# Strassen's seven products in the second MLP matrices of a two-layer decoder trunk, with weight sums formed by accumulating DMAs

## The chip, the core and the metric

The kernel runs on one core of one Trainium2 chip. A core has a matrix engine (TensorE, PE in the profile, with its weight loads as PEld), three engines for elementwise work (VectorE as DVE, ScalarE as ACT, GpSimd as POOL), and SyncE (SP), which here only issues DMAs. DMAs can also be issued from the ACT and POOL queues. The metric is the device time of one execution in microseconds (us); less is better.

## The reference

Two layers over a residual stream x of 256 tokens by 2048 columns, in float32. Layer 0 mixes tokens with gated linear attention, layer 1 with sliding-window attention. Behind each mixer stands the same MLP, with matrices of 2048 x 8192 and 8192 x 2048:

```python
def rmsnorm(x, g):
    xf = x.astype(jnp.float32)
    y = xf * lax.rsqrt(jnp.mean(xf * xf, axis=-1, keepdims=True) + EPS)
    return (y * g.astype(jnp.float32)).astype(x.dtype)

def sqrelu_mlp(h, w1, w2):
    u = jax.nn.relu(h @ w1)
    return (u * u) @ w2

    # in every layer
    h = h + mixer(rmsnorm(h, norm_mix[layer]))
    h = h + sqrelu_mlp(rmsnorm(h, norm_mlp[layer]), mlp_w1[layer], mlp_w2[layer])
```

The change concerns the product with w2, and the square of the ReLU ahead of it. All weights come from HBM once per execution; the four MLP matrices are 256 MiB of them.

## The kernel before: how the work is laid out

**Float32 products by halves.** TensorE is fed with the type float32r. Every float32 operand is split into a high part (a cast) and a low part (what the cast left over), and a product is three matmuls: high x high, high x low, low x high. A weight block of 512 x 512 (1 MiB) is loaded by one DMA from the SP queue into a tile `ws` (`split_w`, line 114; three buffers), and then split in two pieces of 128 x 1024 elements: ScalarE casts to `wh` (line 125), VectorE subtracts to `wl` (line 126). The `wh` and `wl` tiles have four buffers each, which is two blocks. These instructions are put 60 places ahead of program order (`high_priority`), so that blocks are split about two ahead of the matmuls that use them.

**The MLP** (`mlp`, line 666) runs four groups g. A group takes 2048 of the 8192 hidden columns, in two stages:

- The w1 stage: four chunks of 512 hidden columns, each a `gemm_wide` over four blocks (128 matmuls with the weights as the stationary operand). Its result lies hidden column by partition. `evac_u` (line 683) takes it from PSUM: ScalarE copies one half sum and VectorE adds the other (688, 689), GpSimd multiplies by the norm scale of the token (694), VectorE computes max(m, 0) * m (695), ScalarE casts the high part (696) and GpSimd subtracts the low part (697).
- The w2 stage: four chunks of 512 model columns, each a `gemm_mov` over four blocks, 96 matmuls with the activations as the stationary operand: 4 blocks x 4 slices of 128 rows x 2 halves of the tokens x 3. VectorE adds each 128 x 512 result to the residual `xs` (`add_to`, line 621).

The last group of layer 1 (g = 3 without `gains`) has another w2 stage, with weights as the stationary operand, that ends in the output.

**What orders the work.** Program order with those priorities; every engine and every DMA queue executes its instructions in order. `tick` and `later` place small work of one stage between the matmuls of the next. At the end of layer 0 the `add_to` of each chunk also sums squares for the next norm and makes the operands of layer 1 from the chunk a few ticks later.

Of the kernel before, what the change touches and what calls it, by code (L numbers as in the profile page):

```python
# [16 lines left out]
P = 128  # L17
# [31 lines left out]
def yoco_kernel(ctx: ExitStack, tc: tile.TileContext, x, norms, mlp_w1, mlp_w2, a_w_in, w_glr, w_gate, a_g_o, a_w_o,  # L49
# [12 lines left out]
    def bank(shape, tag, dtype=F32):  # L62
        return ps[tag].tile(shape, dtype, name=tag, tag=tag)
# [7 lines left out]
    def later(n, fn):  # L71
        due.setdefault(now[0] + n, []).append(fn)

    def tick():
        now[0] += 1
        for fn in due.pop(now[0], ()):
            fn()

    def mm(o, l, r, start=True, stop=True, **kw):
        nc.tensor.matmul(o, lhsT=l, rhs=r, start=start, stop=stop, **kw)  # L80
# [20 lines left out]
    nc.gpsimd.memset(mhalf, -0.5)  # L101


    def split_w(parts, step=4, queue=nc.sync, between=None):
        ws = wp.tile([P, 4, C], F32, name="ws", tag="ws", bufs=WS)
        halves = [(wp.tile([P, 2, C], F32R, name="wh", tag="wh", bufs=WHL),
                   wp.tile([P, 2, C], F32R, name="wl", tag="wl", bufs=WHL)) for _ in range(2)]
        with tc.high_priority(offset=WPRI):
            for k in range(0, 4, step):
                ks = slice(k, k + step)  # L110
                o = 0
                for ap in parts:
                    n = ap.shape[1]
                    queue.dma_start(out=ws[:, ks, o:o + n],
                                    in_=ap[k * P:(k + step) * P].rearrange("(k p) n -> p k n", p=P))
                    o += n
            n = min(step, 2)
            for k in range(0, 4, n):
                wh, wl = halves[k // 2]
                js, ks = slice(k % 2, k % 2 + n), slice(k, k + n)  # L120
                with ExitStack() as order:
                    if between:
                        for ins in between(k):
                            order.enter_context(tc.issue_after(ins.ins))
                    h = nc.scalar.copy(out=wh[:, js, :o], in_=ws[:, ks, :o])  # L125
                    l = nc.vector.tensor_sub(out=wl[:, js, :o], in0=ws[:, ks, :o], in1=wh.bitcast(F32)[:, js, :o])  # L126
                if between:
                    last[:] = h, l
        return halves
# [156 lines left out]

    last = []

    ss = sm.tile([P, 2, T], F32, name="ss", tag="ss", bufs=1)
    rstd = sm.tile([P, NT], F32, name="rstd", tag="rstd")  # L290
    rb = sm.tile([P, T], F32, name="rb", tag="rb")
    rbq = sm.tile([P, T], F32, name="rbq", tag="rbq", bufs=1)
    rb4, rbq4 = (a.rearrange("p (o t n) -> p o t n", o=1, t=NT).broadcast_to([P, 2, NT, P]) for a in (rb, rbq))
    sqx = []

# [28 lines left out]
        later(8, lambda: nc.scalar.mul(out=rbq, in_=rb, mul=DK ** -0.5))  # L324


    ga = ExitStack()
    gp = ga.enter_context(tc.tile_pool(name="gp", bufs=1))
    g2 = ga.enter_context(tc.tile_pool(name="g2", bufs=2))


# [76 lines left out]
    def two(a, b):  # L408
        return a[:, :, 2 * b:2 * b + 2].rearrange("p t c n -> p c t n")
# [208 lines left out]
    def add_to(c, acts, gains, sq, r):  # L618

        def evac(t, acc):  # L620
            nc.vector.tensor_add(out=xs[c][:, t], in0=acc, in1=xs[c][:, t])
# [44 lines left out]
    def mlp(w1, w2, act, r, gains):  # L666
        mx = ExitStack()
        mp = mx.enter_context(tc.tile_pool(name="mp", bufs=2))
        rb = sm.tile([P, T], F32, name="rb", tag="rb")
        later(RS + 2, lambda: along(rb, r))  # L670
        rb2 = twice(rb)
        sq, nr = new_norm() if gains else (None, None)
        acts = [[] for _ in gains]
        wide_tags.sort()
        for g in range(4):
            us = []
            for c in range(NC4):
                u = new_act()
                us.append(u)

                ms = {}

                def evac_u(f, acc, u=u, ms=ms):
                    ah, al, _ = u
                    if f % 2 == 0:
                        ms[0] = mp.tile([P, 2, T], F32, name="m", tag="m")
                    m, j = ms[0], f % 2
                    nc.scalar.copy(out=m[:, j], in_=acc[:, 1])
                    nc.vector.tensor_add(out=m[:, j], in0=acc[:, 0], in1=m[:, j])  # L689
# [4 lines left out]
                    nc.gpsimd.tensor_mul(out=m, in0=m, in1=rb2)  # L694
                    nc.vector.scalar_tensor_tensor(out=m2, in0=m, scalar=0.0, in1=m, op0=ALU.max, op1=ALU.mult)  # L695
                    nc.scalar.copy(out=ah[:, bs], in_=m2)  # L696
                    nc.gpsimd.tensor_sub(out=al[:, bs], in0=m2, in1=ah.bitcast(F32)[:, bs])  # L697

                go_all(gemm_wide(piece(w1, g * D + c * C), act, evac_u))
            w = w2[g * D:(g + 1) * D]  # L700
# [252 lines left out]
```

## Time and profile before

| | |
|---|---|
| time, median of 3 runs | 2097.48 us (2097.38 to 2099.07) |
| profiled execution | 2099.51 us, with a span of 2097.8 us |
| instructions in the span | 27171 |
| moved by DMA | 381.20 MB, a mean of 182 GB/s |

The span runs from the first to the last instruction; the profiled execution's own time is 1.7 us longer. In the views, a row of a group names the line of the kernel, the engine, the operation, and the output and input tiles with their shapes; its busy time is in us, the mean of one instruction in ns. A matrix-engine instruction is shown from its start to its modelled end, and successive ones overlap, so its duration is more than its share of the time: how long a stage takes is read from the chain of work that ended last, where each piece carries its start, its length and its number of instructions. The view by stretches gives each engine's busy time in a stretch with the number of instructions, then the granted TensorE clock (1.00 is full), the mean busy share of the 16 DMA engines, and GB/s.

### The profile page before, as it was taken

How to read it: one execution, taken by the hardware profiler on the slowest of the kernel's cores; microseconds unless marked ns; L12 is line 12 of the kernel's file. 1: busy time of each engine (PE TensorE's matmuls, PEld its weight loads, DVE VectorE, ACT ScalarE, POOL GpSimd, SP SyncE). 2: the span in 40 equal slices, each digit the busy share in tenths (PEclk: the TensorE clock that was granted, in tenths of full speed). 3: DMA queues.
4: the chain of work that ended last, by engine and by line, in shares of the span. 5: the costliest groups of instructions: out<-in, count | busy, mean ns of one | idle time of the engine just before them, and what ended most of it. 6: DMA issues, size and time to landing. Idle time of an engine off the chain costs nothing.

```text
span 2097.8 us, 27171 instructions
## 1 busy us (share of the span) xinstructions
PE 2086.2 (99%) x10902; PEld 1772.0 (84%) x10902; DVE 1256.8 (60%) x1335; ACT 1017.0 (48%) x1387; POOL 354.4 (17%) x279
## 2 busy tenths in 40 slices
PE   9999999999999999999999999999999999999999
PEld 9988888888888888888888877788888888888888
DVE  6695444566556556645666677566556655655654
ACT  6645445554344434434455677544434434434442
POOL 2262111022012102201300233012102201300310
PEclk9999999999999999999999999999999999999999
DMA  7445555555555655565565433555655565566553
GB/s 277 143 140 180 180 180 163 178 181 195 189 184 195 197 188 194 183 199 184 180 196 186 151 131 123 178 173 191 199 188 193 182 200 184 178 201 199 181 192 130
DMA packets 195871, 381.20 MB, mean 182 GB/s; under 512 B 6577, under 2 KB 14785, under 8 KB 195745
## 3 DMA queue, kind: packets, MB, share of 16 engines
q1 hardware_dynamic: 194704, 377.51, 55.2%
q8 instruction: 85, 1.39, 0.3%
q10 hardware_dynamic: 720, 1.09, 0.2%
q0 software_dynamic: 320, 0.87, 0.2%
q14 instruction: 42, 0.34, 0.0%
HBM read 377.35 MB, written 2.10 MB: 181 GB/s over the span
## 4 chain that ended last, share of the span: by engine, by line
PE 93%; DVE 3%; ACT 2%; DMA 1%; issue 1%; POOL 0%; ACTq 0%; POOLq 0%; DVEq 0%
PE acc L80 70%; PE ms L80 12%; PE tp L80 10%; ACT sc L846 1%; PE tp L605 1%; DVE wl L126 1%; DMA ws<-in_a_w_in_dram 1%; ACT wh L125 1%; PE tp L779 0%; DVE st L840 0%; DVE st L842 0%; PE tp L555 0%; DVE po L868 0%; DVE pv L868 0%; DMA gk<-in_b_g_q_dram 0%
## 5 line engine op out<-in xcount | busy, mean ns | idle before, releaser
L126 DVE TENSOR_TENSOR wl<-ws,wh 128x1024 fp32r<-128x1024 f32 (+1 forms) x720 | 927.0, 1294 | 713.6 <-ACT wh L125 712.7
L125 ACT CAST wh<-ws 128x1024 fp32r<-128x1024 f32 (+1 forms) x720 | 748.1, 1042 | 886.4 <-PE acc L80 676.3
L80 PE MATMUL acc<-wh,act 128*128 128x512 f32 x3136 | 988.0, 392 | 0.0
L80 PEld LDWEIGHTS acc<-wh,act 128*128 128x128 f32 x3136 | 588.0, 188 | 123.8 <-issue 2.0
L80 PE MATMUL acc<-wl,act 128*128 128x512 f32 x1568 | 610.8, 390 | 0.5 <-DVE wl L126 0.5
L80 PE MATMUL acc<-act,wh 128*128 128x512 f32 (+1 forms) x1664 | 412.8, 362 | 1.0 <-ACT wh L125 0.7
L80 PEld LDWEIGHTS acc<-wl,act 128*128 128x128 f32 x1568 | 294.5, 188 | 61.7 <-issue 1.7
L80 PEld LDWEIGHTS acc<-act,wh 128*128 128x128 f32 x1664 | 279.5, 190 | 28.6 <-ACT wh L125 1.0
L80 PE MATMUL acc<-act,wl 128*128 128x256 f32 x1408 | 256.6, 282 | 0.0
L694 POOL TENSOR_TENSOR m<-m,rb 128x512 f32<-128x512 f32 x64 | 81.8, 1300 | 994.5 <-DVE m L689 994.5
L80 PEld LDWEIGHTS acc<-act,wl 128*128 128x128 f32 x1408 | 226.3, 190 | 25.1 <-DVE wl L126 0.3
L80 PE MATMUL tp<-act,wh 128*128 128x512 f32 x592 | 230.1, 394 | 0.0
L80 PE MATMUL ms<-act,wh 128*128 128x512 f32 x576 | 225.9, 394 | 0.0
L80 PE MATMUL ms<-act,wl 128*128 128x256 f32 x576 | 148.6, 281 | 0.0
L80 PE MATMUL tp<-act,wl 128*128 128x256 f32 x576 | 148.3, 280 | 0.0
L697 POOL TENSOR_TENSOR act<-m,act 128x512 fp32r<-128x512 f32 x64 | 130.7, 2057 | 50.2 <-ACT act L696 50.2
L80 PEld LDWEIGHTS tp<-act,wh 128*128 128x128 f32 x592 | 111.5, 189 | 13.3
L80 PEld LDWEIGHTS ms<-act,wh 128*128 128x128 f32 x576 | 108.6, 189 | 13.6
L80 PEld LDWEIGHTS tp<-act,wl 128*128 128x128 f32 x576 | 108.3, 189 | 12.7
L80 PEld LDWEIGHTS ms<-act,wl 128*128 128x128 f32 x576 | 108.5, 189 | 11.9
L695 DVE SCALAR_TENSOR_TENSOR m<-m 128x512 f32<-128x512 f32 x64 | 84.1, 1344 | 26.4 <-POOL m L694 26.4
L696 ACT CAST act<-m 128x512 fp32r<-128x512 f32 x64 | 39.3, 622 | 48.8 <-DVE m L695 48.8
(185 smaller groups left out, 947.2 us busy)
## 6 DMA issues: line engine op xcount, KB each, us to landing
ws<-in_mlp_w_dram SPq DMA_DIRECT2D x256, 1024.0 KB, 5.1
ws<-in_a_w_in_dram SPq DMA_DIRECT2D x44, 1024.0 KB, 5.0
ws<-in_a_w_o_dram SPq DMA_DIRECT2D x16, 1024.0 KB, 4.9
ws<-in_b_w_q_dram SPq DMA_DIRECT2D x16, 1024.0 KB, 5.0
ws<-in_b_w_o_dram SPq DMA_DIRECT2D x16, 1024.0 KB, 5.0
ws<-in_a_w_in_dram SPq DMA_DIRECT2D x12, 256.0 KB, 6.4
xt<-in_x_dram SPq DMA_DIRECT2D x8, 256.0 KB, 6.6
ws<-in_kv_w_k_dram SPq DMA_DIRECT2D x4, 512.0 KB, 4.3
```

Source lines behind the costliest of these rows:

```text
L80: nc.tensor.matmul(o, lhsT=l, rhs=r, start=start, stop=stop, **kw)
L125: h = nc.scalar.copy(out=wh[:, js, :o], in_=ws[:, ks, :o])
L126: l = nc.vector.tensor_sub(out=wl[:, js, :o], in0=ws[:, ks, :o], in1=wh.bitcast(F32)[:, js, :o])
L605: nc.tensor.transpose(out=tp[:, j, t], in_=xs[c][:, t, (2 * b + j) * P:(2 * b + j + 1) * P], identity=ident)
L694: nc.gpsimd.tensor_mul(out=m, in0=m, in1=rb2)
L695: nc.vector.scalar_tensor_tensor(out=m2, in0=m, scalar=0.0, in1=m, op0=ALU.max, op1=ALU.mult)
L696: nc.scalar.copy(out=ah[:, bs], in_=m2)
L697: nc.gpsimd.tensor_sub(out=al[:, bs], in0=m2, in1=ah.bitcast(F32)[:, bs])
L846: nc.scalar.activation(out=sc[:, h], in_=sc[:, h], func=AF.Exp, bias=nmx[:, h:h + 1], scale=f[:, h:h + 1], accum_out=su[:, h:h + 1])
```

## The change

In both MLPs, all groups but the last of layer 1 (seven of eight) have a new w2 stage. It handles the model columns in two halves n of 1024. A half is a 2 x 2 x 2 product of blocks: the two halves of the tokens, two blocks of 512 hidden columns, two of 512 model columns, summed over two pairs q of hidden blocks. Eight half products become seven, by the Strassen-Winograd form:

- **Activations.** `combine` forms the seven left factors of each pair of hidden chunks: three subtractions on VectorE (`less`), and for every factor a cast on ScalarE and a subtraction on VectorE (`half`), all 128 x 512.
- **Weights.** The seven right factors of a pair q come as a chain of sums in place: `X` holds block (0,0), then + (0,1), then + (1,1), then + (1,0); `Y` holds block (1,1), then + (0,1); block (1,0) is used alone. A first block is a plain load from the SP queue. A block is added by a DMA from the GpSimd queue with `accum_op=ALU.add`, into the tile whose last value has just been split. Each of the 14 values is split by `halve`, which is the loop of `split_w` made a function. `X` has two buffers of its own, `Y` and the single block share `ws`.
- **Products.** `product` is 24 matmuls (2 pairs x 4 slices x 3) into one PSUM bank. Its sum is added to one or two of the four 128 x 512 residual tiles or to a tile `v` that is kept over the groups.
- **The ReLU.** VectorE now computes max(m, 0) * rb, with the norm scale rb, and ScalarE squares the result into a float32 tile `u`. GpSimd no longer takes part. In the group that keeps the old w2 stage the low part is subtracted on VectorE.

Besides, two tiles of the first layer's mixer move to a pool that is released before the MLP. The core of the diff; `halve` is the old loop with the same instructions:

```diff
-                m2 = mp.tile([P, 2, T], F32, name="m2", tag="m2")
-                nc.gpsimd.tensor_mul(out=m, in0=m, in1=rb2)
-                nc.vector.scalar_tensor_tensor(out=m2, in0=m, scalar=0.0, in1=m, op0=ALU.max, op1=ALU.mult)
-                nc.scalar.copy(out=ah[:, bs], in_=m2)
-                nc.gpsimd.tensor_sub(out=al[:, bs], in0=m2, in1=ah.bitcast(F32)[:, bs])
+                nc.vector.scalar_tensor_tensor(out=m, in0=m, scalar=0.0, in1=rb2, op0=ALU.max, op1=ALU.mult)
+                nc.scalar.activation(out=uf[c][:, bs], in_=m, func=AF.Square)
...
+        def combine(op, odd, uf):
...
+            def half(i, a):
+                nc.scalar.copy(out=op[i][:, 0], in_=a)
+                nc.vector.tensor_sub(out=op[i][:, 1], in0=a, in1=op[i].bitcast(F32)[:, 0])
...
+            if not odd:
+                half(0, ua[:, :, :P])
+                half(6, less(ua[:, :, :P], ua[:, :, P:]))
+                return
+            e = less(ua[:, :, P:], ub[:, :, P:])
+            s = less(ua[:, :, :P], e)
+            half(4, e)
+            half(2, less(ub[:, :, :P], s))
+            half(5, s)
+            half(1, ub[:, :, :P])
+            half(3, ub[:, :, P:])
...
+            def load(ws, q, i, j):
+                with tc.high_priority(offset=WPRI):
+                    nc.sync.dma_start(out=ws, in_=block(q, i, j))
+                return ws
+
+            def more(ws, q, i, j):
+                with tc.high_priority(offset=WPRI):
+                    nc.gpsimd.dma_start(out=ws, in_=block(q, i, j), accum_op=ALU.add)
+                return ws
...
+            weights = [lambda q: load(new(X, q), q, 0, 0), lambda q: load(new(Y, q), q, 1, 1),
+                       lambda q: more(X[q], q, 0, 1), lambda q: more(Y[q], q, 0, 1), lambda q: more(X[q], q, 1, 1),
+                       lambda q: load(new({}, q), q, 1, 0), lambda q: more(X[q], q, 1, 0)]
...
+            def product(i, b, o):
...
+                for q in range(2):
+                    halves = halve(weights[i](q))
+                    op = ops[q][o]
+                    for k in range(4):
+                        wh, wl = (h[:, k % 2] for h in halves[k // 2])
+                        st = fresh and q == 0 and k == 0
+                        mm(banks[b], op[:, 0, k], wh, st, False, skip_group_check=True)
+                        mm(banks[b], op[:, 0, k], wl, False, False, skip_group_check=True)
+                        mm(banks[b], op[:, 1, k], wh, False, q == 1 and k == 3, skip_group_check=True)
+                    tick()
+                return banks[b]
...
+            p = product(0, "A", 0)
+            if g == 0:
+                nc.scalar.mul(out=v, in_=p, mul=-1.0)
+            else:
+                sub(v, p)
+            add(x12, product(1, "E", 2))
+            p = product(2, "B", 4)
+            add(x12, p)
+            add(x22, p)
+            sub(x22, product(3, "C", 6))
+            add(v, product(4, "D", 5))
+            if final:
+                add(x12, v)
+                add(x22, v)
+                done(c1)
+                sub(x21, v)
+            add(x11, product(5, "A", 1))
+            add(x21, product(6, "C", 3))
+            if final:
+                done(c0)
...
-            if g < 3 or gains:
-                for c in range(NC4):
-                    go_all(gemm_mov(piece(w, c * C), us, add_to(c, acts, gains if g == 3 else (), sq, nr)))
+            if not plain:
+                for n in range(2):
+                    seven(w, n, ops, g, g == 3 or (g == 2 and not gains), acts, gains if g == 3 else (), sq, nr)
                 continue
```

More of the change, by code (lines that the diff above doesn't have):

```diff
@@ L101, in yoco_kernel, with halve @@
     nc.gpsimd.memset(mhalf, -0.5)
+    def halve(ws, o=C, n=2, between=None, low=None):
+        halves = [(wp.tile([P, 2, C], F32R, name="wh", tag="wh", bufs=WHL),
+                   wp.tile([P, 2, C], F32R, name="wl", tag="wl", bufs=WHL)) for _ in range(2)]
+        with tc.high_priority(offset=WPRI):
+            for k in range(0, 4, n):
+                wh, wl = halves[k // 2]
+                js, ks = slice(k % 2, k % 2 + n), slice(k, k + n)
+                with ExitStack() as order:
+                    if between:
+                        for ins in between(k):
+                            order.enter_context(tc.issue_after(ins.ins))
+                    h = nc.scalar.copy(out=wh[:, js, :o], in_=ws[:, ks, :o])
+                    l = (low or nc.vector).tensor_sub(out=wl[:, js, :o], in0=ws[:, ks, :o],
+                                                      in1=wh.bitcast(F32)[:, js, :o])
+                if between:
+                    last[:] = h, l
+        return halves
     def split_w(parts, step=4, queue=nc.sync, between=None):
         ws = wp.tile([P, 4, C], F32, name="ws", tag="ws", bufs=WS)
-        halves = [(wp.tile([P, 2, C], F32R, name="wh", tag="wh", bufs=WHL),
-                   wp.tile([P, 2, C], F32R, name="wl", tag="wl", bufs=WHL)) for _ in range(2)]
         with tc.high_priority(offset=WPRI):
@@ L116, in split_w @@
                     o += n
[L117 to L129, printed above, removed]
+        return halve(ws, o, min(step, 2), between)
     def piece(w, col, n=C):
@@ L287, in yoco_kernel @@
     last = []
[L289 removed]
     rstd = sm.tile([P, NT], F32, name="rstd", tag="rstd")
     rb = sm.tile([P, T], F32, name="rb", tag="rb")
[L292 removed]
+    ga = ExitStack()
+    gp = ga.enter_context(tc.tile_pool(name="gp", bufs=1))
+    ss = gp.tile([P, 2, T], F32, name="ss")
+    rbq = gp.tile([P, T], F32, name="rbq")
     rb4, rbq4 = (a.rearrange("p (o t n) -> p o t n", o=1, t=NT).broadcast_to([P, 2, NT, P]) for a in (rb, rbq))
@@ L674, in mlp, with new_ops, less @@
         wide_tags.sort()
+        vs = [mp.tile([P, C], F32, name=f"v{n}", bufs=1) for n in range(2)]
+        def new_ops():
+            two = lambda: actp.tile([P, 2, 2, 4, P], F32R, name="ops", tag="act")
+            pairs = [two() for _ in range(2)]
+            return [t[:, i] for t in pairs for i in range(2)] + \
+                [mp.tile([P, 2, 4, P], F32R, name=f"op{i}", tag=f"op{i}") for i in range(3)]
+        def combine(op, odd, uf):
+            ua, ub = (uf[c] for c in sorted(uf)[-2:]) if odd else (uf[max(uf)], None)
+            def half(i, a):
+                nc.scalar.copy(out=op[i][:, 0], in_=a)
+                nc.vector.tensor_sub(out=op[i][:, 1], in0=a, in1=op[i].bitcast(F32)[:, 0])
+            def less(a, b):
+                e = mp.tile([P, 4, P], F32, name="e", tag="e")
+                nc.vector.tensor_sub(out=e, in0=a, in1=b)
+                return e
+            if not odd:
[9 more added lines that the diff above has]
+            half(3, ub[:, :, P:])
@@ new lines, in seven, with block, new, done @@
+        def seven(w, n, ops, g, final, acts, gains, sq, nr):
+            c0, c1 = 2 * n, 2 * n + 1
+            x11, x21, x12, x22 = (xs[c][:, t] for c in (c0, c1) for t in range(NT))
+            v = vs[n]
+            X, Y = {}, {}
+            def block(q, i, j):
+                r = (2 * q + i) * C
+                return w[r:r + C, (c0 + j) * C:(c0 + j + 1) * C].rearrange("(k p) n -> p k n", p=P)
+            def load(ws, q, i, j):
[3 more added lines that the diff above has]
+            def more(ws, q, i, j):
+                with tc.high_priority(offset=WPRI):
+                    nc.gpsimd.dma_start(out=ws, in_=block(q, i, j), accum_op=ALU.add)
+                return ws
+            def new(d, q):
+                if d is X:
+                    d[q] = mp.tile([P, 4, C], F32, name="wx", tag="wx")
+                else:
+                    d[q] = wp.tile([P, 4, C], F32, name="ws", tag="ws", bufs=WS)
+                return d[q]
+            weights = [lambda q: load(new(X, q), q, 0, 0), lambda q: load(new(Y, q), q, 1, 1),
+                       lambda q: more(X[q], q, 0, 1), lambda q: more(Y[q], q, 0, 1), lambda q: more(X[q], q, 1, 1),
+                       lambda q: load(new({}, q), q, 1, 0), lambda q: more(X[q], q, 1, 0)]
+            banks = {}
+            def product(i, b, o):
+                fresh = b not in banks
+                if fresh:
+                    banks[b] = bank([P, C], "ms" if b in "DE" else "acc")
+                for q in range(2):
[9 more added lines that the diff above has]
+                return banks[b]
+            add = lambda o, p: nc.vector.tensor_add(out=o, in0=p, in1=o)
+            sub = lambda o, p: nc.vector.tensor_sub(out=o, in0=o, in1=p)
+            def done(c):
+                if not gains:
+                    return
+                for t in range(NT):
+                    junk = sm.tile([P, C], F32, name="junk", tag="junk", bufs=1)
+                    nc.scalar.activation(out=junk, in_=xs[c][:, t], func=AF.Square, accum_out=sq[:, t, c:c + 1])
+                turn.append(c)
+                if len(turn) % 2 == 0:
+                    for i, cc in enumerate(sorted(turn[-2:])):
+                        for b in range(2):
+                            later(1 + 2 * i + b, lambda b=b, cc=cc: operands(acts, gains, cc, b))
+                if len(turn) == NC4:
+                    later(1, lambda: rstd_of(nr, sq))
+            p = product(0, "A", 0)
+            if g == 0:
+                nc.scalar.mul(out=v, in_=p, mul=-1.0)
+            else:
+                sub(v, p)
[14 more added lines that the diff above has]
+                done(c0)
@@ L675, in mlp, with evac_u @@
+        turn = []
         for g in range(4):
-            us = []
+            w = w2[g * D:(g + 1) * D]
+            plain = g == 3 and not gains
+            us, ops, uf = [], [], {}
             for c in range(NC4):
-                u = new_act()
-                us.append(u)
+                if plain:
+                    us.append(new_act())
+                elif c % 2 == 0:
+                    ops.append(new_ops())
                 ms = {}
-                def evac_u(f, acc, u=u, ms=ms):
-                    ah, al, _ = u
+                def evac_u(f, acc, c=c, ms=ms):
@@ L685, in evac_u @@
                     if f % 2 == 0:
                         ms[0] = mp.tile([P, 2, T], F32, name="m", tag="m")
+                    if f == 0:
+                        uf[c] = mp.tile([P, 4, T], F32, name="u", tag="u")
                     m, j = ms[0], f % 2
```

9 lines of the change are left out of this document (6 added, 3 removed).

## The prediction

> **What bounds the kernel now.** I read the page's busy times and the engine shares of its chain first, then the chain piece by piece through one group of layer 0, then the stretches of that group's two stages.
>
> ```profile
> PE 2086.2 (99%) x10902; PEld 1772.0 (84%) x10902; DVE 1256.8 (60%) x1335; ACT 1017.0 (48%) x1387; POOL 354.4 (17%) x279
> PE 93%; DVE 3%; ACT 2%; DMA 1%; issue 1%; POOL 0%; ACTq 0%; POOLq 0%; DVEq 0%
> ```
> ```profile
> 507.51 109.49 PE acc L80 x512
> 639.45 22.45 PE acc L80 x128
> 684.36 109.51 PE acc L80 x512
> ```
> ```profile
> core 0: us, PE busy (x) PEld busy (x) DVE busy (x) ACT busy (x) POOL busy (x), PEclk, DMA share, GB/s
> 507.50:594.50 87.00, 87.00 (x386) 72.01 (x385) 48.23 (x45) 35.45 (x38) 5.67 (x4) 1.00 0.58 190
> 594.50:684.40 89.90, 89.90 (x514) 78.58 (x513) 55.33 (x52) 40.78 (x51) 20.86 (x12) 1.00 0.59 191
> ```
>
> The matrix engine is on the chain for 93% of the span. In the MLP no other engine appears between its instructions: 512 of them follow each other for 109.49 us, which is the w2 stage of a group (384) and the first chunk of the next w1 stage (128). A chunk of w1 takes 22.45, so the w2 stage takes 109.49 - 22.45 = 87.0 us and one of its matmuls 87.04 / 384 = 226.7 ns. The period is 684.36 - 507.51 = 176.9 us: 89.9 for w1, 87.0 for w2. In both stages VectorE is busy for 48 to 55 us and the DMA engines for 0.58 of the time. So fewer matmuls do shorten a w2 stage, until the next resource is full. Which one that is has to be read within this stage; averages over the span hide it.
>
> **What is removed.** A half n of the new stage has 7 x 24 = 168 matmuls where two chunks had 192: 24 x 226.7 ns = 5.44 us less, leaving 38.1 us. The matmuls keep their shape, and already go three in a row into one bank, so I keep their price. Over 2 halves and 7 groups that is 76.2 us: the ceiling of the gain, if everything else hides in 38.1 us per half.
>
> **VectorE and ScalarE in a half.** Rows for the splitting of weights, for the sums into the residual, and for what an activation chunk costs:
>
> ```profile
> L125 ACT CAST wh<-ws x35: 1046/1055/1056, 507.1 to 599.7; 128x1024 fp32r<-128x1024 f32 x35
> L126 DVE TENSOR_TENSOR wl<-ws,wh x34: 1212/1225/1736, 508.1 to 599.4; 128x1024 fp32r<-128x1024 f32 x34
> ```
> ```profile
> L621 DVE TENSOR_TENSOR xs<-acc,xs x72: 680/683/692, 362.1 to 1911.4; 128x512 f32<-128x512 f32 x72
> ```
> ```profile
> L695 DVE SCALAR_TENSOR_TENSOR m<-m x64: 676/1768/1781, 444.2 to 2006.7; 128x512 f32<-128x512 f32 x64
> ```
> ```profile
> L689 DVE TENSOR_TENSOR m<-acc,m 128x256 f32<-128x256 f32 x64 | 22.6, 417 | 0.0
> L126 DVE TENSOR_TENSOR wl<-ws,wh 128x512 fp32r<-128x512 f32 x16 | 10.6, 694 | 4.4 <-ACT wh L125 4.3
> L125 ACT CAST wh<-ws 128x512 fp32r<-128x512 f32 x16 | 9.7, 618 | 4.3 <-DMA ws<-in_a_w_in_dram 4.0
> L694 POOL TENSOR_TENSOR m<-m,rb 128x512 f32<-128x512 f32 x64 | 81.8, 1300 | 994.5 <-DVE m L689 994.5
> L697 POOL TENSOR_TENSOR act<-m,act 128x512 fp32r<-128x512 f32 x64 | 130.7, 2057 | 50.2 <-ACT act L696 50.2
> ```
>
> A half splits 14 weight values, each in two pieces, where two chunks split 8 blocks. VectorE: 28 x 1.225 = 34.3 us, and 8 sums x 0.683 = 5.5, together 39.8 against 38.1 of matmuls. It is as full as TensorE before anything else is asked of it. ScalarE: 28 x 1.055 = 29.5, covered.
>
> What the last w1 chunk leaves for VectorE falls into the same stage: 4 x 0.417 + 2 x 0.676 + 8 x 0.694 (five splits and three differences of the odd pair) = 8.6 us. I take the shortest multiply, 0.676, since the long ones of 1.77 run while GpSimd works (its 1300 ns are gone after the change). VectorE's work in a stage is 2 x 39.8 + 8.6 = 88.2, of which the last two sums (1.4) may run under the next w1 stage: 86.8 us. Work split ahead at the start is repaid at the end. **So VectorE alone takes the 76 us back: 86.8 against 87.0.**
>
> **The w1 stage** stays with TensorE: VectorE's 55.3 us grow by 20 x 0.694 and shrink by 8 x (1.77 - 0.68) to about 60, ScalarE's 40.8 by 14 x 0.618 to 49, of 89.9. There the moved norm scale, the removed 2057 ns subtraction and the square in place of a cast cost and gain nothing: the matmuls cover them. In the group that keeps its old stage likewise. In the final groups three more sums per half (0.69 each) and, at the end of layer 0, the operands of the last two chunks come later; two blocks of the next projection (2 x 24 matmuls, 10.9 us) cover these. Without that cover 8 us and 3 us are lost in all.
>
> **DMA in a half.** Before, 8 loads of 1 MiB; now 6 plain loads and 8 accumulating ones.
>
> ```profile
> 10.00:15.00 5.00, 4.93 (x38) 4.64 (x36) 4.55 (x10) 4.33 (x10) 0.14 (x1) 1.00 1.06 407
> ```
> ```profile
> ws<-in_mlp_w_dram SPq DMA_DIRECT2D x256, 1024.0 KB, 5.1
> wg<-in_w_gate_dram POOLq DMA_DIRECT2D x1, 512.0 KB, 6.1
> gk<-in_b_g_q_dram POOLq DMA_DIRECT2D x1, 32.0 KB, 3.9
> ```
> ```profile
> 6.58 0.77 POOL L350 DMA_DIRECT2D go<-in_a_g_o_dram  x1
> 9.57 0.56 POOL L358 DMA_DIRECT2D wg<-in_w_gate_dram  x1
> ```
>
> With all engines full (share 1.06) the core moved 407 GB/s: 2.58 us per MiB. The trace shows no accumulating DMA. It can't be cheaper than a plain one, 2.58 us, since its bytes come from HBM too. At the upper end stands the row of the same queue, 512 KB landing in 6.1 us: 12.2 us per MiB if such DMAs go one by one. I take twice the plain price, 5.16 us, an estimate: to form out + in, a DMA engine must read the old tile as well as the block. Its tile and row length are those of the plain load, so that row is nearer than the GpSimd rows, taken in the crowd of the start. A half then occupies the DMA engines for 6 x 2.58 + 8 x 5.16 = 56.8 us, 1.5 times its matmuls.
>
> The Trainium skill, "Collectives: The Full Stack", section "The bandwidth ceiling: the fold count and why AG ≠ RS ≠ AR", says that a reduction in the DMA path is slow not for its addition but because it "needs two source reads", and gives 62.28 against 32.35 GB/s, a factor of 1.93. By that the half would take 15.5 + 8 x 4.98 = 55.3 us and the kernel about 2261; no run here shows an accumulation yet.
>
> Can this spread into the w1 stage, whose share is 0.59? Hardly: X has two buffers, Y and the single block use the three of `ws`, and a sum can't be issued before its tile's last value is split. X of the first half and one Y block come early (3 x 2.58 = 7.7 us); at the end the last landing beyond its transfer (5.1 - 2.6), its split (2 x 1.06 + 1.23) and its 12 x 0.2267 us of matmuls stand alone: 8.5 us. These cancel.
>
> New waits: on the GpSimd queue each accumulation waits for VectorE's `wl` of its tile; behind it stand only later accumulations and the norm's small powers. On SP the next half's X waits for the last split of the old one, with Y, the single blocks and the next w1 blocks behind it.
>
> **The sum.** A stage of two halves: 2 x 56.8 = 113.6 us, 26.6 more than 87.0; times 7 groups, +186. The profiled execution took 2099.5, so 2285; the median before is 2.0 lower: **2283 us**.
>
> **Rivals.** One row more for the first of them, a pair of sums in 1.28 us:
>
> ```profile
> 594.12 1.28 DVE L621 TENSOR_TENSOR xs<-acc,xs 128x512 f32<-128x512 f32 x2
> ```
>
> *Accumulations are nearly as cheap as plain loads, and VectorE binds (not slower).* It holds if 12 x 2.58 + 16a stays under 86.8, that is a under 3.5 us, and if sums land in time: a tile of X is due again after 4 steps of 2.72 us less 3.3 for its split, 7.6 us, against 5.1 for a plain landing and 3.9 for the smallest GpSimd one. For it: nothing here shows that the second read costs engine time. Time: 7 x (86.8 - 87.0) = -1, so 2096. With 16 sums at 0.64 us (half of that pair) and 56 splits at their shortest, 1.212, it would be 10 us less, 2086; with 2 us of waiting per stage 2110. Chance 0.19: 0.09 faster, 0.06 same, 0.04 slower.
>
> *The GpSimd queue serves accumulations one by one.* For it: 128 rows occupied it for 0.56 to 0.77 us, and a block has 512 rows. Above 7.1 us each (56.8 / 8) this decides; at 12.2, 2 x 97.6 - 87 = 108 per group, +757, 2855. Against it: 4 x 0.77 = 3.1 us is less than 5.16. Chance 0.19, half of it above 9.9 us, which is 2600.
>
> *The clock drops while TensorE waits.*
>
> ```profile
> 1302.00:1312.00 10.00, 7.66 (x39) 5.76 (x38) 7.71 (x10) 6.11 (x15) 1.90 (x1) 0.97 0.46 154
> ```
>
> With waits in a stretch the granted clock was 0.97. At half clock a half needs 76.2 us: 7 x (152.4 - 87) = +458, 2555. But then TensorE would not wait, and the clock would return. Chance 0.05. The Trainium skill ("TensorE: Matmul & The Clock Gate", "HAM oscillation — how this bites in real kernels") puts the point at idle gaps over about 3.4 us; the trace's 0.97 neither confirms nor excludes that.
>
> **How the numbers follow.** The forecast (0.57) spans a from 3.5 to 7 us, about 2100 to 2490. Of the range, 2086 to 2600, the low end is VectorE's case at its best, the high end a GpSimd queue at 9.9 us; about 0.05 lies below and 0.10 above. A difference under 0.2% (4 us) can't be told from none. Faster 0.09, same 0.06, slower 0.85.
>
> **What would show it.** Right: w2 stages near 113 us with DMA shares near 1, VectorE at 0.75 of them, TensorE at two thirds, ScalarE's casts waiting for accumulations; w1 chunks still at 22.45. Wrong: a DMA share well under 1 with casts waiting (then landing or the queue binds), or VectorE at 95% and stages of 87 us (then the accumulation was mispriced).

## The result and the profile after

| | before | after |
|---|---|---|
| median | 2098.22 us (2097.38 to 2099.07, 4 runs) | 2330.89 us (2329.12 to 2332.82, 4 runs) |
| profiled execution, span | 2099.51, 2097.8 us | 2329.12, 2327.4 us |
| w2 stage, mean of the seven | 87.0 us for six, layer 0's last 90.4 | 118.3 us (117.6 to 119.5) |

The changed kernel takes 1.1109 times as long (95% interval 1.109 to 1.1128). The forecast was 2283 us in a range of 2086 to 2600, slower with a chance of 0.85.

First the page after: the busy times of the engines, and of the DMA queues the packets, MB, and the time that packets took as a share of 16 engines' span.

```profile
PE 2139.3 (92%) x10566; PEld 1756.8 (75%) x10566; DVE 1492.7 (64%) x1729; ACT 1226.5 (53%) x1665; POOL 289.0 (12%) x263
...
q1 hardware_dynamic: 179920, 348.15, 44.4%
q0 software_dynamic: 59456, 118.32, 28.4%
...
L116 ACT CAST wh<-wx 128x1024 fp32r<-128x1024 f32 x224 | 227.8, 1046 | 305.1 <-DMA wx<-in_mlp_w_dram 241.6
...
L732 POOL DMA_DIRECT2D wx<-in_mlp_w_dram x84 | 108.1, 1287 | 1240.2 <-DVE wl L117 1052.1
...
ws<-in_mlp_w_dram SPq DMA_DIRECT2D x200, 1024.0 KB, 5.2
wx<-in_mlp_w_dram POOLq DMA_DIRECT2D x84, 1024.0 KB, 11.5
...
ws<-in_mlp_w_dram POOLq DMA_DIRECT2D x28, 1024.0 KB, 13.7
```

TensorE has 336 fewer instructions and is still "busy" for 53 us more. That is no work: part of it ran at half clock, as shown below. What is new stands in the queue rows. All 112 accumulating DMAs are on q0: they bring a quarter of the bytes (118.32 of 469 MB) and take 28.4% of the engines' span, against 44.4% for three times as many. They land after 11.5 and 13.7 us where a plain 1 MiB block takes 5.2, and ScalarE's casts of `wx` wait 241.6 us for them.

Next the view by stretches: two w2 stages, the w1 stage between them, and three short pieces of the first w2 stage. (After the engines' busy times come clock, DMA share, GB/s.)

```profile
508.10:627.60 119.50, 95.67 (x339) 71.20 (x338) 78.18 (x81) 61.69 (x69) 19.24 (x15) 0.87 1.05 237
717.40:835.50 118.10, 95.27 (x338) 70.19 (x338) 79.86 (x83) 61.02 (x67) 19.26 (x15) 0.87 1.05 237
627.60:717.40 89.80, 89.80 (x514) 78.47 (x513) 57.83 (x68) 44.61 (x60) 1.29 (x1) 1.00 0.62 201
...
532.00:540.00 8.00, 8.00 (x37) 6.62 (x36) 5.86 (x5) 3.89 (x4) 0.85 (x1) 1.00 1.11 230
544.00:550.00 6.00, 5.33 (x13) 4.17 (x14) 6.00 (x7) 3.47 (x5) 1.28 (x1) 0.50 1.12 208
552.00:558.00 6.00, 6.00 (x29) 4.95 (x27) 3.03 (x4) 1.74 (x2) 0.00 (x0) 1.00 1.07 308
```

The w2 stage went from a DMA share of 0.58 to 1.05, the share at which the engines were full at the start of the kernel before (1.06). It holds in the short pieces as well, whatever TensorE does there. VectorE is busy for 65% of the stage, ScalarE for 52%. The w1 stage is still TensorE's alone, at full clock. Read the two kinds of row together: the bound has moved to the DMA engines, and only in the stage that was changed.

One wait in that stage, from TensorE's timeline and from ScalarE's (start, length, instruction, idle time before it and its releaser):

```profile
543.41 0.50 PE L80 MATMUL ms<-wh,op 128*128 128x512 f32 x1 [2.51 <-ACT wh L116]
544.67 0.79 PE L80 MATMUL ms<-wl,op 128*128 128x512 f32 x1 [0.76 <-DVE wl L117]
```
```profile
542.31 1.99 ACT L116 CAST wh<-wx 128x1024 fp32r<-128x1024 f32 x2 [4.91 <-DMA wx<-in_mlp_w_dram]
```

TensorE waits 2.51 us for a cast, and the cast has waited 4.91 us for an accumulation to land. The page's chain of waits breaks off in this kernel, so I read the chain in neighbouring kernels below.

**Where the 229.6 us of span are.** The seven stages take 827.9 us for 612.6: +215. From layer 0's last w2 stage to the first one of layer 1 it is 350.6 for 341.9: +8.7. The other w1 stages give about +3 and the last group, which keeps its old stage, +2.

### The profile page after: what moved, and what is told of

Read it like the earlier page. It is cut to its first block, busy times and chain, and to the rows that moved or that the text cites. A ratio compares the mean times of both kernels' runs of the same rounds, so it can differ in the third digit from the quotient of the medians.

```text
span 2327.4 us, 27349 instructions
## 1 busy us (share of the span) xinstructions
PE 2139.3 (92%) x10566; PEld 1756.8 (75%) x10566; DVE 1492.7 (64%) x1729; ACT 1226.5 (53%) x1665; POOL 289.0 (12%) x263
## 3 DMA queue, kind: packets, MB, share of 16 engines
q1 hardware_dynamic: 179920, 348.15, 44.4%
q0 software_dynamic: 59456, 118.32, 28.4%
## 5 line engine op out<-in xcount | busy, mean ns | idle before, releaser
L80 PE MATMUL acc<-wh,act 128*128 128x512 f32 x1344 | 434.8, 397 | 0.0
L117 DVE TENSOR_TENSOR wl<-wx,wh 128x1024 fp32r<-128x1024 f32 x224 | 269.2, 1222 | 223.6 <-ACT wh L116 223.1
L116 ACT CAST wh<-wx 128x1024 fp32r<-128x1024 f32 x224 | 227.8, 1046 | 305.1 <-DMA wx<-in_mlp_w_dram 241.6
L80 PEld LDWEIGHTS acc<-wh,act 128*128 128x128 f32 x1344 | 252.3, 188 | 53.8 <-issue 2.0
L80 PE MATMUL acc<-wl,act 128*128 128x512 f32 x672 | 262.8, 391 | 0.0
L732 POOL DMA_DIRECT2D wx<-in_mlp_w_dram x84 | 108.1, 1287 | 1240.2 <-DVE wl L117 1052.1
L80 PE MATMUL acc<-wh,ops 128*128 128x512 f32 x672 | 226.0, 409 | 24.3 <-ACT wh L116 21.7
L80 PE MATMUL acc<-wh,op 128*128 128x512 f32 x448 | 159.8, 427 | 24.6 <-ACT wh L116 19.2
L80 PEld LDWEIGHTS acc<-wh,ops 128*128 128x128 f32 x672 | 134.0, 199 | 60.4 <-ACT wh L116 28.2
L80 PE MATMUL acc<-wl,ops 128*128 128x512 f32 x336 | 139.5, 415 | 14.9 <-DVE wl L117 14.7
L80 PEld LDWEIGHTS acc<-wl,act 128*128 128x128 f32 x672 | 126.7, 189 | 26.4 <-issue 1.7
## 6 DMA issues: line engine op xcount, KB each, us to landing
wx<-in_mlp_w_dram POOLq DMA_DIRECT2D x84, 1024.0 KB, 11.5
ws<-in_mlp_w_dram POOLq DMA_DIRECT2D x28, 1024.0 KB, 13.7
```

Of the source, the lines that this page charges most:

```text
L117: l = (low or nc.vector).tensor_sub(out=wl[:, js, :o], in0=ws[:, ks, :o], in1=wh.bitcast(F32)[:, js, :o])
L732: nc.gpsimd.dma_start(out=ws, in_=block(q, i, j), accum_op=ALU.add)
```

## The experiments

Theory: an accumulating DMA takes two passes of DMA engine time, and in the w2 stage these engines are full. Rivals: the GpSimd queue or the landing time of each sum in the chain of X; VectorE, which on paper fills 87 us by itself; the half clock after waits. "The sums" are the additions of weight blocks.

**The same loads, without the addition**, on the same queue (`plain_pool`), then on SP (`plain_sp`):

```diff
-                    nc.gpsimd.dma_start(out=ws, in_=block(q, i, j), accum_op=ALU.add)
+                    nc.gpsimd.dma_start(out=ws, in_=block(q, i, j))     # plain_pool
+                    nc.sync.dma_start(out=ws, in_=block(q, i, j))       # plain_sp
```

> Each accumulating DMA becomes a plain load of the same block into the same tile from the same GpSimd queue (the sums of weight blocks are left out). Engine theory (an accumulating packet occupies a DMA engine for 178 ns where a plain one takes 92, from the queues' shares in the changed kernel): the DMA work of a half falls from 63 to 41 us, VectorE binds, w2 stages of 87 to 93 us instead of 119, time 2100 to 2145. Queue theory (the GpSimd queue and its late landing of 11.5 us are the cost, not the addition): landing stays above 9 us, stages stay above 110 us, time above 2265.

> The same plain loads, but issued from the SP queue (sums left out). Engine theory: as the plain loads from the GpSimd queue, within 1%, 2100 to 2145. Queue theory: much shorter than those from the GpSimd queue, near 2100, while those stay above 2265. VectorE as the next limit: VectorE busy for over 93% of a w2 stage in this run.

Measured: `plain_pool` 2138.97 us, ratio to before 1.0192 [1.0175, 1.0209]; `plain_sp` 2105.95, 1.0039 [1.0027, 1.0052]. Stages 90.9 and 86.9 us in the mean. The first stage of each by stretches, and rows of the page of `plain_pool`:

```profile
508.60:596.50 87.90, 79.92 (x339) 63.67 (x338) 77.81 (x81) 63.10 (x69) 11.25 (x15) 0.98 0.88 314
```
```profile
508.60:595.80 87.20, 81.24 (x339) 64.91 (x338) 78.93 (x82) 63.71 (x69) 0.00 (x0) 0.96 0.85 305
```
```profile
q0 software_dynamic: 30784, 118.32, 15.8%
...
wx<-in_mlp_w_dram POOLq DMA_DIRECT2D x84, 1024.0 KB, 5.4
```

The same bytes on the same queue, only not added: 82% of the loss is gone (191.9 of 232.7 us), the landing falls from 11.5 to 5.4 us, q0's share of engine time from 28.4% to 15.8%. So the queue one by one is not the cause. It costs something all the same: on SP the kernel is 33 us faster still, 1.6%, where I had said within 1%. VectorE was busy for 90.5% of the stage on SP, where my sign for it as the next limit was over 93%. With both away 97% of the loss is gone. What remains is 2106, not 2022: the 76 us of saved matmuls do not come back.

**Half the sums** (`half_sums`): the second and third additions to X, which make its third and fourth value, become plain SP loads.

```diff
+            again = load
-                       lambda q: more(X[q], q, 0, 1), lambda q: more(Y[q], q, 0, 1), lambda q: more(X[q], q, 1, 1),
-                       lambda q: load(new({}, q), q, 1, 0), lambda q: more(X[q], q, 1, 0)]
+                       lambda q: more(X[q], q, 0, 1), lambda q: more(Y[q], q, 0, 1), lambda q: again(X[q], q, 1, 1),
+                       lambda q: load(new({}, q), q, 1, 0), lambda q: again(X[q], q, 1, 0)]
```

> Of the 8 accumulating DMAs of a half, the 4 first stay and the 4 into the third and fourth value of X become plain loads from the SP queue (those sums are left out). Engine theory: the DMA work of a half is 10 x 2.94 + 4 x 5.69 = 52.2 us at a full share of 1.05, a stage of 99 us, time 2190 (2165 to 2215). A theory in which the chain of X sets the time (three accumulations in a row, each landing late): two of the three links are gone, stages near 87 to 92, time below 2140.

Measured: 2230.33 us, 1.0626 [1.061, 1.0642]; stages 104.5.

```profile
508.60:613.50 104.90, 88.54 (x338) 67.77 (x337) 79.29 (x83) 62.56 (x69) 8.96 (x7) 0.92 0.97 270
```

Half the additions, about half the loss: midway between 2106 and 2331 is 2218. It is above what I expected (99 us a stage, 2190), and the DMA share is 0.97 and not 1.05, so some of this stage is waiting and not engine time. The chain of X as what sets the time by itself, which would have given under 2140, falls.

**Keep TensorE at full clock** (`fill_waits`, `fill_two`): matmuls of no use ahead of each step of a product, six or two of 512 columns, into a spare bank.

```diff
+                    spare = bank([P, C], "tp")
+                    for _ in range(FILL):
+                        mm(spare, identr, op[:, 0].rearrange("p k n -> p (k n)"))
```

> The changed kernel, with 6 more matmuls of 512 columns ahead of each of the 14 steps of a half (19 us of matmuls per half, into a bank that nobody reads), so that TensorE is not idle for long while it waits for weights. Engine theory: the DMA engines stay the limit and TensorE has the room (2 x 57 = 114 us in a stage of 119): granted clock back to 0.98 or more, time 2331 within 1.5%. Clock theory (the half clock after waits, 0.87 on average in a stage, lengthens the stages): time falls by 2% or more, below 2285.

> The changed kernel with 2 more matmuls of 512 columns ahead of each step (in place of 6, which filled TensorE to 97%). Engine theory: DMA stays the limit, 2331 within 0.5%, whatever the clock does. Clock theory: granted clock of a stage above 0.93 and time below 2310.

Measured: six, 2364.65 us, 1.1266 [1.1249, 1.1283]; two, 2344.65, 1.1174 [1.1159, 1.119]. The first stage with six and the first two with two:

```profile
508.30:631.20 122.90, 118.56 (x507) 95.51 (x506) 80.23 (x83) 62.59 (x69) 19.24 (x15) 0.99 1.04 240
```
```profile
508.50:631.70 123.20, 105.64 (x394) 79.73 (x393) 79.40 (x82) 62.08 (x69) 19.25 (x15) 0.90 1.01 230
721.50:842.80 121.30, 104.39 (x394) 79.02 (x393) 80.81 (x85) 61.33 (x67) 19.27 (x15) 0.92 1.03 234
```

With six the clock is back at 0.99 and nothing is won; but TensorE itself is full there (118.56 of 122.90), so this run alone excludes little. With two it has 17 us free and the clock is 0.90 to 0.92 where it was 0.87, and the stage is a little longer still. The kernel is 0.6% above the changed one, where I had said within 0.5%, and the clock reached less than I wanted for a clean test (0.93). But it moved up, and the time did not move down.

**Take work from VectorE**, with the accumulations as they are (`sums_less_low`) and with plain SP loads (`plain_sp_less_low`): the low parts of the last three of seven weight values are left out, and the high part is multiplied in their place. That removes 24 of 56 subtractions in a stage.

```diff
-                    halves = halve(weights[i](q))
+                    halves = halve(weights[i](q), low="none" if i > 3 else None)
...
-                        mm(banks[b], op[:, 0, k], wl, False, False, skip_group_check=True)
+                        mm(banks[b], op[:, 0, k], wl if i < 4 else wh, False, False, skip_group_check=True)
```

> The changed kernel with its accumulating DMAs, but without the low parts of the last 3 weight values (their second matmul takes the high part): 24 of 56 splits less on VectorE in a stage, the DMAs as they are. Engine theory: the DMA engines hold the stage at 118 us whatever VectorE does, 2331 within 0.7%. If VectorE's queue delays the accumulations (each waits for a low part), time falls by over 1%, below 2307.

> Plain loads from the SP queue again (sums left out), and the low parts of the last 3 of the 7 weight values are not formed: their second matmul takes the high part, so TensorE has as many matmuls as before. VectorE has 24 of 56 splits less in a stage. VectorE theory (with the DMA cost gone, VectorE holds the stage at 87 us): stages of 78 to 82 us, near the matmuls' 76, time 2045 to 2075. Theory of waits (not VectorE's work but landings or the four buffers of the halves hold it): stages still above 84, time 2090 to 2106.

Measured: with accumulations 2318.71 us, 1.1044 [1.1025, 1.1062], which is 0.5% less than the changed kernel; with plain loads 2096.27, 0.9987 [0.9978, 0.9996]. The chain of `sums_less_low` is whole, by engine and line; of the other kernel the first of these lines, and its first stage:

```profile
PE 63%; DMA 22%; DVE 6%; ACT 4%; issue 4%; POOL 1%; ACTq 0%; POOLq 0%; SPq 0%; DVEq 0%
PE acc L80 41%; DMA wx<-in_mlp_w_dram 21%; PE ms L80 12%; PE tp L80 9%; DVE wl L119 3%; ACT wh L117 2%; ACT sc L982 1%; DMA ws<-in_mlp_w_dram 1%; PE tp L612 1%; DMA ws<-in_kv_w_k_dram 0%; POOL wx L734 0%; DVE e L701 0%; PE tp L915 0%; DMA ws<-in_a_w_in_dram 0%; DVE st L976 0%
```
```profile
PE 87%; DVE 6%; ACT 3%; DMA 1%; issue 1%; POOL 0%; SPq 0%; ACTq 0%; POOLq 0%; DVEq 0%
```
```profile
509.17:594.38 85.21, 79.34 (x339) 63.90 (x337) 51.69 (x58) 63.66 (x69) 0.00 (x0) 0.98 0.87 312
```

Two readings. With accumulations the chain lies on the landing of `wx` for 21% of the span, and on VectorE for 6%. The 24 subtractions were worth 12 of the 233 us: VectorE is not a main term of the loss. With plain loads the stage is 85.2 us although VectorE is busy for only 51.7 of them, where `plain_sp` had 87.2 with 78.9. By the theory of VectorE I had expected 78 to 82 us and 2045 to 2075; the theory of waits, over 84 us and 2090 to 2106, came in. So the theory that VectorE's throughput gives the 76 us back, mine and on record, falls too: it was 91% busy, and taking a third of its work away bought (2105.95 - 2096.27) / 7 = 1.4 us a stage.

What holds that stage can be read from its chain of waits in order of time. Of `plain_sp_less_low`:

```profile
509.33 4.12 PE acc L80 x18
...
513.48 1.06 ACT wh L117
...
522.54 0.60 DVE ops L697
523.14 0.67 DVE op L697 x2
...
524.26 0.69 DVE e L701
...
524.98 0.63 ACT ops L696
...
525.65 1.22 PE ms L80 x2
...
554.50 0.57 issue
555.08 1.23 DVE wl L119
...
556.35 5.55 PE acc L80 x23
```

Between 513.5 and 525.7 us no piece of the chain is TensorE's: the last hidden chunk of the w1 stage is being turned into the left factors (casts, splits, differences), and TensorE cannot finish the second product without them. TensorE's own waits there are shorter, 4.1 us (1.18, 0.74 and 2.20), since it works meanwhile on what needs no late factor. The other break is at 554.5, the half boundary, where X is loaded anew: here TensorE waits 1.69 us for a split of the new X, which stands behind a sum in VectorE's order; in the chain of `plain_sp` a landing of `wx` of 5.20 us stands at that place. These waits are 5.8 us of the 9.0 by which the stage is longer than 76.2; in the rest, its matmuls were slower (the clock is 0.98).

**The head of the stage earlier** (`plain_sp_early`): as the last one, and products 1 and 2 take their first pair q = 0, whose chunks are long done, both before q = 1.

```diff
-            add(x12, product(1, "E", 2))
-            p = product(2, "B", 4)
+            product(1, "E", 2, (0,))
+            product(2, "B", 4, (0,))
+            add(x12, product(1, "E", 2, (1,)))
+            p = product(2, "B", 4, (1,))
```

> As the run with plain SP loads and without the low parts of the last 3 weight values (sums and low parts left out), but the first pair of hidden blocks takes its step in the products 1 and 2 before the second pair does. In the run without this, VectorE's work on the last hidden chunk is done 16 us after the stage begins, and TensorE has 8.2 us of work that doesn't need it; now it has 10.9 us. Head theory (what is left above the matmuls' 76 us is the wait for the last chunk's factors at the head of a stage): stages fall from 86 by about 2.7 to 5.4 us, time 2058 to 2078. Theory of buffers or landings all along the stage: no change, 2090 to 2100.

Measured: 2096.73 us, 0.9992 [0.9979, 1.0005]: a miss for the theory of the head. The chain of its first stage shows where the gain went:

```profile
522.68 1.22 PE acc L80 x4
...
549.28 4.86 DMA wx<-in_mlp_w_dram
...
556.57 5.39 DMA wx<-in_mlp_w_dram
```

TensorE resumes in the chain at 522.7 and not 525.7, in a stage that began 1.1 us earlier, but its own waits at the head fall only from 4.1 us to 3.5 (2.33, 0.43 and 0.71). Then two landings of X stand in the chain at the half boundary, where it waits 2.1 us instead of 1.7. The head alone is not the limit, and the reload of X takes over. More buffers for X were not tried, so how far the stage goes with both waits away stays open.

**The low parts on GpSimd** (`plain_sp_gps_low`): plain SP loads, and 14 of the 56 low parts of a stage are subtracted on GpSimd.

```diff
-                    l = (low or nc.vector).tensor_sub(out=wl[:, js, :o], in0=ws[:, ks, :o],
+                    l = (low or {}).get(k, nc.vector).tensor_sub(out=wl[:, js, :o], in0=ws[:, ks, :o],
...
-                    halves = halve(weights[i](q))
+                    halves = halve(weights[i](q), low={2: nc.gpsimd} if q else None)
```

> Plain loads from the SP queue (sums left out), and 14 of the 56 low parts of a stage are formed on GpSimd instead of VectorE. If the two engines work side by side, VectorE is relieved by 17 us and stages fall to 80 to 84 us: time 2060 to 2090. If a subtraction of two tiles on VectorE is held up while GpSimd reads two tiles (before the change VectorE's multiply took 1.77 us beside GpSimd and 0.68 without): no gain, 2100 or more.

Measured: 2191.86 us, 1.0441 [1.0408, 1.0474]; stages 92 to 103, a mean of 97.4 for 86.9. Of my two forecasts, 2060 to 2090 if the engines work side by side and 2100 or more if they collide, the second came in. Rows of the tile `wl` in its first w2 stage (least, median, longest ns):

```profile
L117 DVE TENSOR_TENSOR wl<-ws,wh x20: 1209/1214/3284, 513.2 to 601.3; 128x1024 fp32r<-128x1024 f32 x20
L117 POOL TENSOR_TENSOR wl<-wx,wh x8: 2407/2914/4594, 510.3 to 596.8; 128x1024 fp32r<-128x1024 f32 x8
```

GpSimd needs 2.4 us at best, and when both subtract, single instructions take 2.7 times the least on VectorE and 1.9 times on GpSimd. The Trainium skill ("SBUF — State Buffer", "Who interferes with whom") has it that this operation on VectorE contends with GpSimd's reads when both its inputs lie in SBUF; these rows agree. How much of the stage's 10 us is this, and how much GpSimd's slower subtraction, is not separated.

**The sums bought as two plain loads** (`twice_plain`): each accumulation becomes two SP loads of its block into the same tile.

```diff
-                    nc.gpsimd.dma_start(out=ws, in_=block(q, i, j), accum_op=ALU.add)
+                    nc.sync.dma_start(out=ws, in_=block(q, i, j))
+                    nc.sync.dma_start(out=ws, in_=block(q, i, j))
```

> Each accumulating DMA becomes two plain loads of its block from the SP queue, one after the other into the same tile (sums left out). No addition, no GpSimd queue, but twice the plain engine time, as an accumulation has (178 against 84 to 92 ns a packet). Engine theory (an accumulation costs what two passes of a block cost): DMA work of a half 6 x 2.94 + 16 x 2.94 = 65 us at a share of 1.05, stages of 118 to 124 us, time 2325 to 2365. If the addition or the GpSimd queue costs something of its own, clearly less: below 2290.

Measured: 2423.96 us, 1.1533 [1.15, 1.1566]; stages 132.2. Its first stage, and the waits of the SP queue (total us, times, longest):

```profile
508.50:640.00 131.50, 97.03 (x337) 72.19 (x337) 80.48 (x82) 62.06 (x69) 0.00 (x0) 0.86 0.93 340
```
```profile
SPq L733 <- DMA wx<-in_mlp_w_dram: 423.3, 84, 8.2
```

The time is above my 2325 to 2365. The engine time is that of the accumulations, 0.93 x 131.5 = 122 us against 1.05 x 119.5 = 125. But the second load waits for the first to land, 423.3 us in all, with the other loads of SP behind it. As a test of the time it is inconclusive; in engine time, an accumulation comes to what two loads of its block take.

**The norm scale alone** (`norm_only`): the kernel before with the changed ReLU and nothing else.

```diff
-                    nc.gpsimd.tensor_mul(out=m, in0=m, in1=rb2)
-                    nc.vector.scalar_tensor_tensor(out=m2, in0=m, scalar=0.0, in1=m, op0=ALU.max, op1=ALU.mult)
+                    nc.vector.scalar_tensor_tensor(out=m, in0=m, scalar=0.0, in1=rb2, op0=ALU.max, op1=ALU.mult)
+                    nc.scalar.activation(out=m2, in_=m, func=AF.Square)
...
-                    nc.gpsimd.tensor_sub(out=al[:, bs], in0=m2, in1=ah.bitcast(F32)[:, bs])
+                    nc.vector.tensor_sub(out=al[:, bs], in0=m2, in1=ah.bitcast(F32)[:, bs])
```

> The kernel before with the new handling of the ReLU alone: norm scale in VectorE's instruction, square on ScalarE, low part on VectorE, GpSimd out of it. Theory of the prediction: hidden under the matmuls, within 0.2% of before, 2094 to 2102. Rival: a shorter or longer tail of a w1 stage shows at the stages' boundaries, more than 0.2% either way.

Measured: 2098.28 us, 0.9997 [0.9988, 1.0006]. It costs and gains nothing; TensorE covers it.

## Why the prediction was right, point by point

- **The accumulating DMA at twice a plain load, the DMA engines as the bound: right.** The queue rows give it per packet: 28.4% x 16 x 2327.4 / 59456 = 178 ns for 2 KB on q0, 44.4% x 16 x 2327.4 / 179920 = 92 ns on q1, 1.94 times. The page "Collectives: The Full Stack" of the Trainium skill gave 1.93 for a reduction, in its section on the fold count; the trace agrees. (The time that I worked out by that page, 2261, comes to 2263 by its own terms.) That the second half of the time is the reading of the old tile, as I argued, no run shows.
- **The price, 5.16 us per MiB: right. The size, 113.6 us a stage: a term was missing.** Four stretches of the changed kernel, behind each of the first two the row of the only queue that moved weights in it (packets, MB, share), and an issue from GpSimd's timeline:

```profile
516.00:532.00 16.00, 11.81 (x37) 8.23 (x36) 12.62 (x17) 9.19 (x14) 3.82 (x3) 0.79 1.13 205
q0 software_dynamic: 1634, 3.25, 112.1%
558.00:562.00 4.00, 2.23 (x7) 1.24 (x6) 2.62 (x3) 1.99 (x2) 0.00 (x0) 0.86 1.05 410
q1 hardware_dynamic: 818, 1.64, 105.3%
562.00:572.00 10.00, 7.97 (x28) 5.64 (x27) 6.57 (x8) 5.75 (x6) 1.29 (x2) 0.88 0.55 145
771.40:781.40 10.00, 7.49 (x25) 5.42 (x24) 7.47 (x9) 6.09 (x6) 2.57 (x2) 0.83 0.58 147
```
```profile
568.34 1.28 POOL L732 DMA_DIRECT2D wx<-in_mlp_w_dram  x1 [20.41 <-DMA wx<-in_mlp_w_dram]
```

  Accumulations alone run at 205 GB/s, which is 5.1 us per MiB, plain loads alone at 410, which is 2.6. So 12 plain loads and 16 accumulations are 12 x 2.6 + 16 x 5.1 = 113 us, as forecast. But at the half boundary the share falls to 0.55 and 0.58 for 10 us, about 5 us of unused engines in each of these two stages, and in the other five it is 0.49 to 0.62 at the same place: no accumulation into the new X can be issued before X has landed and been split (GpSimd's next one comes 20.41 us after its last). 113 and 5 are 118 of the measured 118.3. This is an estimate: a block's worth of loading falls outside the stage (237 GB/s x 119.5 us are 27.0 MiB and not 28), and a shorter gap lies inside. My working names this wait, the next half's X behind the last split of the old one, and gives it no time. The stages grew by 215 us and not 186: 29 of the 48 us between forecast and median are this.
- **"Without that cover 8 us and 3 us are lost in all": it was lost.** I let two blocks of the next projection cover the late operands at the end of layer 0. Of the 8.7 us there, this is the largest wait, from TensorE's timeline after and the first 20 us behind the stage in both kernels, after and before:

```profile
1270.30 1.09 PE L610 MATMUL tp<-ident,xs 128*128 128x128 f32 x4 [5.68 <-DVE act L243]
```
```profile
1252.80:1272.80 20.00, 13.48 (x58) 10.34 (x58) 13.38 (x23) 9.81 (x20) 8.07 (x12) 0.87 0.52 158
```
```profile
1128.60:1148.60 20.00, 20.00 (x93) 16.55 (x92) 13.40 (x20) 11.87 (x19) 0.73 (x1) 1.00 0.58 196
```

- **"So VectorE alone takes the 76 us back: 86.8 against 87.0": the number came out, the reason did not.** With plain loads on SP the stage is 86.9 us and the kernel 2106, in the range of that rival. But without 24 of its 56 subtractions it is 86. The rows counted VectorE as full at 88; in that stage it was busy for 79, and what holds the stage above the 76 us of its matmuls are mostly two waits, for the left factors of the last chunk and at the reload of X. A sum of an engine's work that equals the stage is no proof that this engine binds.
- **The queue one by one: wrong as the bound,** but the GpSimd queue is not free: 33 us over SP with plain loads.
- **The clock: came in, and in the changed kernel cost nothing that was seen.** In the stretches, it is 0.50 in the piece behind TensorE's 2.51 us wait and 1.00 in the pieces on both sides. The Trainium skill ("TensorE: Matmul & The Clock Gate", "HAM oscillation — how this bites in real kernels") speaks of idle gaps over about 3.4 us; the trace differs. The clock is 1.00 from 543.0 to 543.5, 0.83 in the next half microsecond and 0.50 after it: it dropped before the wait of 0.76, which begins at 543.91, so the wait of 2.51 us and the start of one matmul were enough. TensorE waits for its weights anyway, so slower pieces would only shorten its waits; the runs with useless matmuls, where the clock rose and the time did not fall, fit this.
- **The w1 stage and the moved norm scale: right** (89.8 us of 89.8 busy; `norm_only` 0.9997). VectorE was at 0.65 of the stage and not 0.75, since the stage was longer and its work shorter than I had it. TensorE's 336 matmuls, at full clock 76.2 us, are 0.64 of 118.3, the two thirds I named.

No variant here beats the kernel before by more than 0.13%. Even with the sums for nothing, which no longer computes the product, it is 2106 us against 2098, and 2096 to 2097 with a part of the low halves left out as well.

## What to carry to other kernels

When a scheme trades matmuls for sums of operands, count what each operand costs before it reaches the matrix engine: here one product in eight was saved, and 14 weight values had to be loaded and split where there were 8. An accumulating DMA took twice the engine time of a plain load here, so price it so and compare the sum with the stage in which it runs, not with the span. Then look where a chain of such sums starts anew: the engines that bind stood nearly idle there. And before you call an engine the bound because its work fills the stage, take a third of that work away and look.

## What the runs showed of the hardware

- An accumulating DMA from HBM into SBUF takes packets of 2 KB at 178 ns; a plain load issued by GpSimd went in 30784 packets for the same bytes, about 4 KB each, at 15.8% x 16 x 2137.1 / 30784 = 175 ns. So the addition halves the packet and keeps its time.
- The issue of one accumulating block on GpSimd occupies it for 1.29 us (108.1 / 84).
- VectorE's instructions follow each other faster than their durations say. In the chain of `plain_sp`, one after the other in a busy piece:

```profile
517.25 1.13 DVE wl L117
518.39 0.60 DVE m L825
518.99 1.14 DVE wl L117
```

The 128x1024 subtraction counts 1.13 us there and the 128x512 multiply 0.60, where I had taken 1.225 and, for a 128x512 one, 0.68 to 0.69 each. For the subtractions, which are most of VectorE's bill, that is 8% less.
